# The first projection stage of a hybrid decoder layer: three output tiles instead of two beside the loads of x

## The chip, the cores and the metric

The kernel runs on one core of a Trainium2 chip. The core has a matrix engine (TensorE, PE in the profile), a vector engine (VectorE, DVE), a scalar engine (ScalarE, ACT), a general engine (GpSimd, POOL) and a queue engine (SyncE, SP). Transfers between HBM and the on-chip memory (SBUF) are issued by SP, ACT or POOL and carried out by 16 DMA engines. TensorE writes its results to PSUM, a small memory of eight banks, from where ACT and DVE read them. The metric is the device time of one execution in microseconds (us).

## The reference

One decoder layer: 16 meta tokens are put in front of 512 tokens, so that 528 positions of 1024 channels go in; 512 come out, in float32. What matters here is its first step, the normalization and the input projection, and what the first state-space group takes from it.

```python
h = jnp.concatenate([meta, x], axis=1)            # 528 x 1024
u = rmsnorm(h, mix_norm_w[i])                     # h * rsqrt(mean(h*h) + eps) * w
proj = u @ w_in[i]                                # 1024 x 9248 weights
u_pool = proj[..., OFF_POOL:OFF_Z]
z      = proj[..., OFF_Z:OFF_XBC]
xbc    = proj[..., OFF_XBC:OFF_DT]                # x (2048), B (1024), C (1024)
dt_raw = proj[..., OFF_DT:OFF_GATE]               # 32 heads
gates  = jax.nn.sigmoid(proj[..., OFF_GATE:] + b_gate[i])
...
xbc = jax.nn.silu(causal_depthwise_conv(xbc, conv_w, conv_b))
dt  = jax.nn.softplus(dt_raw + dt_bias)
...  # pooling branch, state-space scan over chunks of 128, gated merge, w_o, squared-ReLU MLP
out = rmsnorm(h, final_norm_w)
```

## The kernel before, in words

**Layout.** Positions run along the free axis: x comes in transposed as `in_xT`, eight tiles `xt[k]` of 128 channels by 528 positions (264 KB each). The weights lie in HBM as a list of blocks of 128 by 1024 float32 (512 KB), in the order in which the kernel takes them; a block of the input projection is one output tile, 128 output channels, with its eight contraction pieces of 128 columns side by side. One vector table, `in_vec` (128 by 234, 117 KB), holds all small per-channel numbers; its first eight columns are `mix_norm_w`.

**Split operands.** Each float32 operand of a matmul is split in two: ACT makes a rounded high part (`xh`, `whi`) and DVE the rest (`xl`, `wlo`). A product then takes three matmuls: high by high (line 149), high weight by low x (line 150), low weight by high x (line 152). `block_part` loads a range of columns of a block on SP's queue and splits it (lines 79 and 80). Three tiles of raw weights (tag `raw`) and four pairs of split weights can be live.

**First stage (lines 182 to 251).** x isn't normalized yet: `x_split` (lines 203 and 204) multiplies it by `mix_norm_w` only, and the results are multiplied by the row scale `rsb` afterwards (`first_raw`, line 378). While the eight tiles `xt[k]` arrive, TensorE accumulates two output tiles of group 0, B and C, in two-bank PSUM tiles `pB` and `pC` (the pool `psa`, two such tiles): step k takes 12 matmuls of 264 or 258 columns. Their weights come in column ranges 0 to 256, 256 to 512 and 512 to 1024. Before the first data TensorE is kept at work by `WARM` = 9 matmuls on a tile of ones (line 196). `dt_step` (line 212), four contraction pieces for the 32 dt columns, runs behind k = 3 and behind k = 7. The squares of x are summed in `q` beside it.

**Behind it.** dt is gathered (`pdv`, line 258), the sums of squares are taken over channels (`pn`, line 275) and turned into the row scale `rsb` (lines 279 to 295), which the softplus chain for dt, the two first-stage results and all later products of unnormalized x wait for. TensorE goes on with the rest of group 0: the tiles 0 and 1 of x (lines 390 and 391), z (`pz`), and four gate tiles (`pgp`). z is taken out of PSUM by DVE with the row scale (line 402). Then `norm_u` has made the normalized, split `uh` and `ul` (lines 353 to 355), and the groups follow. One-bank PSUM tiles come from the pool `psb` (four tiles): `pdt`, `pdv`, `pn`, `pb1`.

**Order.** The framework's planner sets the order of the work on each engine. It goes through the program with a model of times of its own: of the instructions that its model holds to be ready, an engine takes the one that stands first in the program. Each engine then works its list off in that order, so an instruction that waits holds up those behind it on its engine. The load of the activation tables of ACT stands right ahead of ACT's first ACTIVATE.

Of the kernel before, what the change touches and what calls it, by code (L numbers as in the profile page):

```python
# [9 lines left out]
F32 = mybir.dt.float32  # L10
F32R = mybir.dt.float32r
AF = mybir.ActivationFunctionType
ALU = mybir.AluOpType

P = 128
# [3 lines left out]
L = SEQ + NM  # L19
HALF = L // 2  # L20
NK = D // P
# [13 lines left out]
V_MIX, V_BG, V_PS, V_CW, V_CB, V_DS, V_SN, V_MN, V_DTB, V_AL = (  # L35
    0, 8, 24, 32, 160, 192, 208, 224, 232, 233)
# [6 lines left out]
MERGE = (0, 4, 1, 5, 2, 6, 3, 7)  # L43

WO_ORDER = [(q, i) for q in ("b11", "b12", "b22") for i in range(2)]
WARM = 9


@with_exitstack
def kernel(ctx: ExitStack, tc, xT, x, w, vec, fnw, out):  # L50
    nc = tc.nc
    act, dve, pe, pool = nc.scalar, nc.vector, nc.tensor, nc.gpsimd

    const = ctx.enter_context(tc.tile_pool(name="const", bufs=1, side="left"))
# [8 lines left out]
    def block_tiles():  # L63
        b = nblk[0]
        nblk[0] += 1
        return (b, wp.tile([P, 1024], F32, tag="raw", name=f"raw{b}", bufs=3),
                wp.tile([P, 1024], F32R, tag="whi", name=f"whi{b}"),
                wp.tile([P, 1024], F32R, tag="wlo", name=f"wlo{b}"))

    def block_load(t, c):  # L70
        nc.sync.dma_start(t[1][:, c], w[t[0], :, c])

    def block_part(t, c):
        block_load(t, c)
        block_split(t, c)

    def block_split(t, c):
# [24 lines left out]
    make_identity(nc, ident)  # L102
    ones_r = const.tile([P, P], F32R, name="ones_r")
    ones_f = const.tile([P, P], F32, name="ones_f")
    dve.memset(ones_f, 1.0)
    dve.tensor_copy(ones_r, ones_f)
    tri = const.tile([P, P], F32, name="tri")
    pool.affine_select(out=tri, in_=ones_f, compare_op=ALU.is_ge, fill=0.0, base=0,
                       pattern=[[1, P]], channel_multiplier=-1)
# [3 lines left out]
    eps = const.tile([P, 1], F32, name="eps")  # L113
    dve.memset(eps, EPS)
    vs = const.tile([P, V_N], F32, name="vs")
    nc.scalar.dma_start(vs, vec)

    def col(off, i, n=P):
        return vs[:n, off + i : off + i + 1]
# [19 lines left out]
    def psum2(name):  # L139
        return psa.tile([P, 1024], F32, tag="mm", name=name)  # L140

    def psum1(name):
        return psb.tile([P, 512], F32, tag="s", name=name)

    def proj_step(outs, k, wblk, rhs):

        wh, wl = (t[:, k * P : (k + 1) * P] for t in wblk)
        for o, c in outs:
            pe.matmul(o, wh, rhs[0][k][:, c], start=k == 0, stop=False)  # L149
            pe.matmul(o, wh, rhs[1][k][:, c], start=False, stop=False)  # L150
        for o, c in outs:
            pe.matmul(o, wl, rhs[0][k][:, c], start=False, stop=k == NK - 1)  # L152
# [5 lines left out]
    def wide(ps, skip=0):  # L158

        h = (L - skip) // 2  # L160
        runs = [(ps[:, 512 - h : 512], slice(skip, skip + h)),
                (ps[:, 512 : 512 + h], slice(skip + h, L))]
        return runs, ps[:, 512 - h : 512 + h]

    def narrow(ps):
        return [(ps, slice(NM, L))]
# [3 lines left out]
    xt = [pre.tile([P, L], F32, name=f"xt{k}") for k in range(NK)]  # L170

    xh = [pre.tile([P, 64 + SEQ], F32R, name=f"xh{k}")[:, 64 - NM :] for k in range(NK)]
    xl = [pre.tile([P, 64 + SEQ], F32R, name=f"xl{k}")[:, 64 - NM :] for k in range(NK)]
# [3 lines left out]
    X, U = (xh, xl), (uh, ul)  # L177
    H = HEADS
# [2 lines left out]

    HF = (slice(0, HALF), slice(HALF, L))
    pdt = [psum1(f"pdt{i}") for i in range(2)]
    pB, pC = psum2("px0_16"), psum2("px0_24")
    (runsB, viewB), (runsC, viewC) = wide(pB), wide(pC, NM - 4)
    b = nblk[0]
    nblk[0] += 1
    wdt = pre.tile([P, NK, H], F32, name="wdt")
    wB, wC = block_tiles(), block_tiles()
    e32 = pre.tile([P, H], F32, name="e32")  # L190
    dve.tensor_tensor(e32, ident[:, :H], ident[:, H : 2 * H], op=ALU.add)
    for c in (2, 3):
# [1 line left out]

    for n in range(WARM):
        pe.matmul(pdt[1].rearrange("p (a b) -> p a b", a=4), ones_r,
                  ones_r.unsqueeze(1).to_broadcast([P, 4, P]), start=True, stop=True)

    def x_load(k):
        nc.sync.dma_start(xt[k], xT[:, k, :])  # L200

    def x_split(k):
        act.activation(xh[k], xt[k], AF.Copy, scale=col(V_MIX, k))
        dve.scalar_tensor_tensor(xl[k], xt[k], col(V_MIX, k), xh[k].bitcast(F32),
                                 op0=ALU.mult, op1=ALU.subtract)

    def dt_step(kb):

        for i, run in enumerate(HF):
            for c in range(4):  # L210
                k = kb + c
                pe.matmul(pdt[i][c * H : (c + 1) * H, :HALF], wdt[:, k, :], xt[k][:, run],
                          start=kb == 0, stop=kb == 4, skip_group_check=True)

    def bc_step(k):
        proj_step(runsB, k, wB[2:], X)
        proj_step(runsC, k, wC[2:], X)

    x_load(0)
    x_split(0)  # L220
    for t in (wB, wC):
        block_part(t, slice(0, 256))
    x_load(1)
    bc_step(0)
    x_split(1)
    x_load(2)
    for t in (wB, wC):
        block_part(t, slice(256, 512))
    bc_step(1)
    def square(k):  # L230
        if k == 0:
            act.activation(q, xt[k], AF.Square)
        else:
            s = pre.tile([P, L], F32, tag="sq", name=f"sq{k}", bufs=2)
            act.activation(s, xt[k], AF.Square)
            dve.tensor_tensor(q, q, s, op=ALU.add)

    for k in range(2, NK):
        if k > 2:
            x_load(k)  # L240
        x_split(k)
        if k == 2:
            nc.sync.dma_start(wdt.rearrange("p k h -> p (k h)"), w[b, :, : NK * H])
            dve.tensor_tensor(wdt, wdt, vs[:, V_MIX : V_MIX + NK].unsqueeze(2).to_broadcast([P, NK, H]), op=ALU.mult)
        if k == 4:
            for t in (wB, wC):
                block_part(t, slice(512, 1024))
        bc_step(k)
        if k % 4 == 3:
            dt_step(k - 3)  # L250
        square(k - 2)
    dts_ = pre.tile([P, L], F32, name="dtp")
    for i, run in enumerate(HF):
        act.copy(dts_[:, run], pdt[i][:, :HALF])
# [34 lines left out]
    for i in range(2):  # L289
        pb = psum1(f"pb1_{i}")  # L290
        c = slice(3 * i, 3 * i + 3)
# [14 lines left out]
    for c in range(4):  # L306
        r = slice(c * H, (c + 1) * H)
# [19 lines left out]
    for c in (slice(0, P), slice(P, W)):  # L327
        n = c.stop - c.start
# [29 lines left out]
    def conv(dst, src, ct):  # L358
        n = dst.shape[-1]
        e = src.shape[-1] - n  # L360
        act.activation(dst, src[:, e:], AF.Identity, bias=col(V_CB, ct), scale=col(V_CW, ct * 4 + 3))
        for j in range(1, 4):
            o = max(0, j - e)
            dve.scalar_tensor_tensor(dst[:, o:], src[:, e + o - j : e + n - j],  # L364
                                     col(V_CW, ct * 4 + 3 - j), dst[:, o:], op0=ALU.mult, op1=ALU.add)
        act.activation(dst, dst, AF.Silu)
# [5 lines left out]
        zt = gc.tile([P, 2, SEQ], F32, tag="zt", name=f"zt{g}", bufs=1)  # L372
        return xc, bt, ct, zt

    def first_raw(name, ps, skip):
        r = pre.tile([P, L - skip], F32, tag="raw0", name=f"raw0_{name}", bufs=4)
        act.copy(r, ps)
        dve.tensor_tensor(r, r, rsb[:, skip:], op=ALU.mult)
        return r

    def group_proj(g, cur, gate=None):

        first = g == 0
        xc, bt, ct, zt = cur
        for dst, t, skip in ((bt, 16 + g, 0), (ct, 24 + g, NM - 4), (xc[:, 0, :], 2 * g, 0),
                             (xc[:, 1, :], 2 * g + 1, 0)):
            if first and (dst is bt or dst is ct):
                view = viewB if dst is bt else viewC
            else:
                runs, view = wide(psum2(f"px{g}_{t}"), skip)  # L390
                proj(runs, block(), X if first else U)
            conv(dst, first_raw(t, view, skip) if first else view, t)
            yield
        if gate is not None:
            gate_pool(gate)
            yield
        ps = psum2(f"pz{g}")
        for i in range(2):
            proj(narrow(ps[:, i * SEQ : (i + 1) * SEQ]), block(), X if first else U)
        zf = zt.rearrange("p i t -> p (i t)")  # L400
        if first:
            dve.tensor_tensor(zt, ps.rearrange("p (i t) -> p i t", i=2),
                              rsb[:, NM:].unsqueeze(1).to_broadcast([P, 2, SEQ]), op=ALU.mult)
            act.activation(zf, zf, AF.Silu)
        else:
            act.activation(zf, ps, AF.Silu)
        yield
# [251 lines left out]
    for d in range(NK):  # L659
        ps = psum2(f"psl{d}")[:, :SEQ]  # L660
# [97 lines left out]
    first = []  # L758
    for n, d in enumerate(MERGE):
# [6 lines left out]
        ps = psum2(f"pup{d}")[:, :SEQ]  # L766
        wh, wl = block()
        for i, k in enumerate(ks):
            c = slice(k * P, (k + 1) * P)
# [294 lines left out]
    c = NC - 1  # L1064
# [172 lines left out]
```

## Time and profile before

| | us |
|---|---|
| median of 3 runs (lowest to highest) | 1023.1 (1022.98 to 1023.2) |
| the profiled execution's own time | 1023.79 |
| its span, from the first to the last instruction | 1021.8 |
| PE busy in that span | 1013.0 |
| DVE, ACT busy | 739.7, 550.6 |

A row of the timeline has the start in us, the length in us (of all its instructions, where it stands for several), the engine, the line, the operation with the tiles it writes and reads, its shape, how many there are, and in brackets how long the engine had stood idle before it and for whom. Matmuls are pipelined: one of them takes longer than the distance to the next one, and the distance is what adds up.

### The profile page before, as it was taken

What the parts mean: (1) busy time and instruction counts of PE and PEld (TensorE: products, weight loads), DVE (VectorE), ACT (ScalarE), POOL (GpSimd) and SP (SyncE); (2) the same over time, 40 slices, a digit from 0 to 9 for tenths busy, and PEclk for the clock granted to TensorE, in tenths of its full rate; (3) what the DMA queues carried; (4) which work ended last, traced back from release to release, by engine and by line L of the source; (5) the groups of instructions that cost most, each with busy time, mean ns of one, the idle gap of its engine ahead of it and who ended that gap; (6) DMA issues with size and microseconds to landing.
All of it is one profiled execution on the core that took longest, in us unless ns stands there. A gap on an engine that the chain in (4) does not pass through costs nothing.

```text
span 1021.8 us, 14071 instructions
## 1 busy us (share of the span) xinstructions
PE 1013.0 (99%) x5697; PEld 872.7 (85%) x5697; DVE 739.7 (72%) x988; ACT 550.6 (54%) x729; POOL 10.0 (1%) x24
## 2 busy tenths in 40 slices
PE   9999999999999999999999999999999999999997
PEld 7889888999889998988899888888888888888886
DVE  7987796877836677978765456986686686776866
ACT  8664959495727329473244342475545455454444
POOL 0000000000000000000000001000000000000000
PEclk9999999999999999999999999999999999999999
DMA  7252141505233321514532333224323323324112
GB/s 244 83 164 83 43 145 42 166 21 165 71 95 124 103 91 34 163 26 142 186 103 83 104 104 127 79 93 155 104 83 109 118 82 114 96 101 124 42 42 83
DMA packets 29713, 105.62 MB, mean 103 GB/s; under 512 B 3345, under 2 KB 4689, under 8 KB 28625
## 3 DMA queue, kind: packets, MB, share of 16 engines
q1 hardware_dynamic: 26928, 92.75, 28.1%
q0 software_dynamic: 2000, 11.08, 3.1%
q8 instruction: 45, 0.74, 0.3%
q10 hardware_dynamic: 720, 0.91, 0.3%
q14 instruction: 20, 0.16, 0.0%
HBM read 102.55 MB, written 2.16 MB: 102 GB/s over the span
## 4 chain that ended last, share of the span: by engine, by line
PE 98%; DMA 1%; DVE 1%; ACT 0%; issue 0%; SPq 0%; ACTq 0%
PE px L149 6%; PE px L150 6%; PE px L152 6%; PE pf L98 6%; PE pf L96 6%; PE pf L97 6%; PE alpha L986 3%; PE alpha L988 3%; PE alpha L987 3%; PE pz L149 3%; PE pz L150 3%; PE pz L152 3%; PE py L500 2%; PE pso L96 2%; PE pp L150 2%; PE pp L152 2%
## 5 line engine op out<-in xcount | busy, mean ns | idle before, releaser
L79 ACT CAST whi<-raw 128x1024 fp32r<-128x1024 f32 (+1 forms) x134 | 136.0, 1024 | 232.6 <-PE pf L97 58.8
L80 DVE TENSOR_TENSOR wlo<-raw,whi 128x1024 fp32r<-128x1024 f32 (+1 forms) x134 | 159.0, 1189 | 121.0 <-ACT whi L79 113.7
L149 PE MATMUL px<-uh,whi 128*128 128x264 f32 (+1 forms) x448 | 121.0, 290 | 0.7 <-DVE ct L364 0.7
L150 PE MATMUL px<-ul,whi 128*128 128x264 f32 (+1 forms) x448 | 119.2, 286 | 0.0
L96 PE MATMUL pf<-vh,whi 128*128 128x512 f32 x256 | 99.8, 390 | 0.0
L98 PE MATMUL pf<-vh,wlo 128*128 128x512 f32 x256 | 99.6, 389 | 0.0
L97 PE MATMUL pf<-vl,whi 128*128 128x512 f32 x256 | 99.6, 389 | 0.0
L152 PE MATMUL px<-uh,wlo 128*128 128x264 f32 (+1 forms) x448 | 90.8, 284 | 0.0
L149 PEld LDWEIGHTS px<-uh,whi 128*128 128x128 f32 x448 | 84.6, 189 | 2.7 <-issue 2.4
L150 PEld LDWEIGHTS px<-ul,whi 128*128 128x128 f32 x448 | 84.9, 189 | 0.4 <-issue 0.2
L152 PEld LDWEIGHTS px<-uh,wlo 128*128 128x128 f32 x448 | 69.4, 188 | 0.3 <-issue 0.3
L748 DVE TENSOR_TENSOR slo<-b,shi 128x1024 fp32r<-128x1024 f32 x35 | 42.8, 1222 | 31.6 <-ACT shi L747 31.6
L747 ACT CAST shi<-b 128x1024 fp32r<-128x1024 f32 x35 | 36.8, 1050 | 51.8 <-PE pf L97 36.5
L97 PEld LDWEIGHTS pf<-vl,whi 128*128 128x128 f32 x256 | 48.1, 188 | 10.0
L98 PEld LDWEIGHTS pf<-vh,wlo 128*128 128x128 f32 x256 | 48.0, 188 | 10.0
L96 PEld LDWEIGHTS pf<-vh,whi 128*128 128x128 f32 x256 | 48.0, 188 | 9.9
L986 PE MATMUL alpha<-shi,hh 128*128 128x512 f32 x140 | 54.6, 390 | 0.0
L987 PE MATMUL alpha<-slo,hh 128*128 128x512 f32 x140 | 54.5, 389 | 0.0
L988 PE MATMUL alpha<-shi,hl 128*128 128x512 f32 x140 | 54.5, 389 | 0.0
L813 DVE TENSOR_TENSOR ht<-ht,alpha 128x1024 f32<-128x1024 f32 x35 | 42.6, 1217 | 6.1 <-PE alpha L988 6.1
L149 PE MATMUL pz<-uh,whi 128*128 128x512 f32 x112 | 44.0, 393 | 0.0
L150 PE MATMUL pz<-ul,whi 128*128 128x512 f32 x112 | 43.8, 391 | 0.0
(409 smaller groups left out, 2434.2 us busy)
## 6 DMA issues: line engine op xcount, KB each, us to landing
raw<-in_w SPq DMA_DIRECT2D x128, 512.0 KB, 3.6
b<-in_w SPq DMA_DIRECT2D x28, 512.0 KB, 3.5
abc<-acs_d POOLq DMA_DIRECT2D x8, 1024.0 KB, 7.5
wob<-in_w SPq DMA_DIRECT2D x8, 512.0 KB, 4.5
xt<-in_xT SPq DMA_DIRECT2D x8, 264.0 KB, 5.5
ht<-in_x POOLq DMA_DIRECT2D x4, 512.0 KB, 7.0
w<-in_w SPq DMA_DIRECT2D x4, 512.0 KB, 3.4
out_dram<-out SPq DMA_DIRECT2D x4, 320.0 KB, 2.4
```

Source lines behind the costliest of these rows:

```text
L79: act.copy(hi[:, c], raw[:, c])
L80: dve.tensor_tensor(lo[:, c], raw[:, c], hi[:, c].bitcast(F32), op=ALU.subtract)
L96: pe.matmul(ps, ah, bh, start=first, stop=False)
L97: pe.matmul(ps, ah, bl, start=False, stop=False)
L98: pe.matmul(ps, al, bh, start=False, stop=last)
L149: pe.matmul(o, wh, rhs[0][k][:, c], start=k == 0, stop=False)
L150: pe.matmul(o, wh, rhs[1][k][:, c], start=False, stop=False)
L152: pe.matmul(o, wl, rhs[0][k][:, c], start=False, stop=k == NK - 1)
L748: dve.tensor_tensor(lo, src, hi.bitcast(F32), op=ALU.subtract)
L986: pe.matmul(ps[t], a[0], wh[:, cs], start=f, stop=False, skip_group_check=True)
L987: pe.matmul(ps[t], a[0], wl[:, cs], start=False, stop=False, skip_group_check=True)
L988: pe.matmul(ps[t], a[1], wh[:, cs], start=False, stop=l, skip_group_check=True)
```

## The change: what it does

- A third output tile, tile 0 of x in group 0, is accumulated in the first stage together with B and C, in two one-bank tiles `pX` of `psb`. The x tiles of group 0 that were left for later are then only tile 1; `first_raw` takes a list of views, since the third tile lies in two banks.
- The weights of the three tiles come in ranges of one, one, two and four contraction pieces (64, 64, 128 and 256 KB each), at k = 0, 1, 2 and 4. The first three ranges are issued on ACT's queue, the others on SP's.
- The first x tile is loaded and split in two halves of 264 positions.
- `mix_norm_w` comes as a tile `vm` of its own (4 KB), first on ACT's queue; the whole table `vs` is loaded behind the first weight ranges.
- The load of the dt weights moves to k = 4, and both `dt_step`s behind k = 7.
- The tile of ones is set directly instead of being copied, and `WARM` goes from 9 to 7.

```diff
-WARM = 9
+WARM = 7
...
-    def block_load(t, c):
-        nc.sync.dma_start(t[1][:, c], w[t[0], :, c])
-
-    def block_part(t, c):
-        block_load(t, c)
+    def block_part(t, c, eng=None):
+        (eng or nc.sync).dma_start(t[1][:, c], w[t[0], :, c])
         block_split(t, c)
...
+    dve.memset(ones_r.bitcast(F32), 1.0)
     dve.memset(ones_f, 1.0)
-    dve.tensor_copy(ones_r, ones_f)
...
     vs = const.tile([P, V_N], F32, name="vs")
-    nc.scalar.dma_start(vs, vec)
+    vm = const.tile([P, NK], F32, name="vm")
+    nc.scalar.dma_start(vm, vec[:, V_MIX : V_MIX + NK])
...
-    pB, pC = psum2("px0_16"), psum2("px0_24")
+    pB, pC, pX = psum2("px0_16"), psum2("px0_24"), [psum1(f"px0_0{i}") for i in range(2)]
...
+    runsX = [(pX[i][:, :HALF], HF[i]) for i in range(2)]
...
-    wB, wC = block_tiles(), block_tiles()
+    wBCX = [block_tiles() for _ in range(3)]
...
-    def x_load(k):
-        nc.sync.dma_start(xt[k], xT[:, k, :])
+    def x_load(k, c=slice(0, L)):
+        nc.sync.dma_start(xt[k][:, c], xT[:, k, c])
...
+    def x_split(k, c=slice(0, L)):
+        act.activation(xh[k][:, c], xt[k][:, c], AF.Copy, scale=vm[:, k : k + 1])
+        dve.scalar_tensor_tensor(xl[k][:, c], xt[k][:, c], vm[:, k : k + 1], xh[k][:, c].bitcast(F32),
                                  op0=ALU.mult, op1=ALU.subtract)
...
+    PARTS = {0: slice(0, P), 1: slice(P, 2 * P), 2: slice(2 * P, 4 * P), 4: slice(4 * P, 8 * P)}
...
-    for k in range(2, NK):
-        if k > 2:
-            x_load(k)
-        x_split(k)
-        if k == 2:
+    for k in range(NK):
+        for c in HF if k == 0 else (slice(0, L),):
+            x_load(k, c)
+        if k in PARTS:
+            for t in wBCX:
+                block_part(t, PARTS[k], nc.scalar if k == 0 else nc.sync)
+        if k == 0:
+            nc.scalar.dma_start(vs, vec)
+        if k == 4:
             nc.sync.dma_start(wdt.rearrange("p k h -> p (k h)"), w[b, :, : NK * H])
...
-        bc_step(k)
-        if k % 4 == 3:
-            dt_step(k - 3)
-        square(k - 2)
+        for c in HF if k == 0 else (slice(0, L),):
+            x_split(k, c)
+        for t, runs in zip(wBCX, (runsB, runsC, runsX)):
+            proj_step(runs, k, t[2:], X)
+        if k >= 2:
+            square(k - 2)
+    for kb in (0, 4):
+        dt_step(kb)
...
-    def first_raw(name, ps, skip):
+    def first_raw(name, views, skip):
         r = pre.tile([P, L - skip], F32, tag="raw0", name=f"raw0_{name}", bufs=4)
-        act.copy(r, ps)
+        n = (L - skip) // len(views)
+        for i, o in enumerate(views):
+            act.copy(r[:, i * n : (i + 1) * n], o)
         dve.tensor_tensor(r, r, rsb[:, skip:], op=ALU.mult)
...
-            if first and (dst is bt or dst is ct):
-                view = viewB if dst is bt else viewC
+            if first and t != 1:
+                views = [viewB] if dst is bt else [viewC] if dst is ct else [o for o, _ in runsX]
```

More of the change, by code (lines that the diff above doesn't have):

```diff
@@ L197 @@
                   ones_r.unsqueeze(1).to_broadcast([P, 4, P]), start=True, stop=True)
-    def x_load(k):
[L200 to L204, printed above, removed]
+    def x_load(k, c=slice(0, L)):
[3 more added lines that the diff above has]
+        dve.scalar_tensor_tensor(xl[k][:, c], xt[k][:, c], vm[:, k : k + 1], xh[k][:, c].bitcast(F32),
                                  op0=ALU.mult, op1=ALU.subtract)
@@ L213, in dt_step @@
                           start=kb == 0, stop=kb == 4, skip_group_check=True)
[L215 to L229, printed above, removed]
+    PARTS = {0: slice(0, P), 1: slice(P, 2 * P), 2: slice(2 * P, 4 * P), 4: slice(4 * P, 8 * P)}
     def square(k):
@@ L236, in square @@
             dve.tensor_tensor(q, q, s, op=ALU.add)
-    for k in range(2, NK):
-        if k > 2:
-            x_load(k)
-        x_split(k)
-        if k == 2:
[L243 to L247, printed above, removed]
-        bc_step(k)
-        if k % 4 == 3:
-            dt_step(k - 3)
-        square(k - 2)
+    for k in range(NK):
[7 more added lines that the diff above has]
+        if k == 4:
+            nc.sync.dma_start(wdt.rearrange("p k h -> p (k h)"), w[b, :, : NK * H])
+            dve.tensor_tensor(wdt, wdt, vm.unsqueeze(2).to_broadcast([P, NK, H]), op=ALU.mult)
+        for c in HF if k == 0 else (slice(0, L),):
[6 more added lines that the diff above has]
+        dt_step(kb)
     dts_ = pre.tile([P, L], F32, name="dtp")
@@ L391, in group_proj @@
                 proj(runs, block(), X if first else U)
-            conv(dst, first_raw(t, view, skip) if first else view, t)
+                views = [view]
+            conv(dst, first_raw(t, views, skip) if first else view, t)
             yield
```

## The prediction, written before the changed kernel was run

> **What bounds the kernel now.** I read the page's first part, then what TensorE (PE) waited for, then the timeline of the first 55 us.
>
> ```profile
> span 1021.8 us, 14071 instructions
> PE 1013.0 (99%) x5697; PEld 872.7 (85%) x5697; DVE 739.7 (72%) x988; ACT 550.6 (54%) x729; POOL 10.0 (1%) x24
> ...
> PE pdt L196 <- DVE ones_r L106: 1.5, 1, 1.5
> PE px L149 <- DVE ct L364: 0.7, 1, 0.7
> PE px L150 <- DVE xl L204: 0.4, 1, 0.4
> PE px L149 <- ACT xh L203: 0.2, 1, 0.2
> PE py L500 <- issue: 0.2, 1, 0.2
> ```
>
> TensorE bounds it. The change removes no product, so it can gain only where TensorE waits, or works on nothing useful, at the head. The list of waits shows 0.6 us in the first stage, but a busy PE isn't a PE at its pace; starts show more.
>
> ```profile
> 1.51 0.79 PE L196 MATMUL pdt<-ones_r 128*128 128x512 f32 x1 [1.51 <-DVE ones_r L106]
> ...
> 4.23 0.98 PE L196 MATMUL pdt<-ones_r 128*128 128x512 f32 x2
> 4.66 0.79 PE L196 MATMUL pdt<-ones_r 128*128 128x512 f32 x2
> 5.55 0.69 PE L149 MATMUL px<-xh,whi 128*128 128x264 f32 x2
> ...
> 13.24 1.10 PE L212 MATMUL pdt<-xt,wdt 128*32 128x264 f32 x16
> ...
> 15.83 0.28 PE L149 MATMUL px<-xh,whi 128*128 128x264 f32 x1
> ...
> 18.73 0.28 PE L149 MATMUL px<-xh,whi 128*128 128x264 f32 x1
> ...
> 20.26 1.10 PE L212 MATMUL pdt<-xt,wdt 128*32 128x264 f32 x16
> 21.29 0.39 PE L149 MATMUL px<-xh,whi 128*128 128x264 f32 x1
> ...
> 28.60 0.28 PE L149 MATMUL px<-xh,whi 128*128 128x264 f32 x1
> ...
> 35.17 0.40 PE L149 MATMUL pz<-xh,whi 128*128 128x512 f32 x1
> ...
> 53.34 0.39 PE L149 MATMUL pgp<-xh,whi 128*128 128x512 f32 x1
> ```
>
> Steps 5 and 6 of B and C take 18.73 - 15.83 = 2.90, so a fed step is 1.45 us. The first four, from 5.55 to the first dt step at 13.24, take 7.69 where 5.80 would do: **1.89 us lost**, all to late x and weights. A tile of 264 columns takes (35.17 - 28.60) / 9 = 0.73 per contraction piece, so a step of three tiles is 2.18, and a dt step is 21.29 - 20.26 = 1.03.
>
> ```profile
> 0.81 0.41 ACTq L116 DMA_DIRECT2D vs<-in_vec  x1
> 1.25 0.89 SPq L71 DMA_DIRECT2D raw<-in_w  x2
> 1.25 1.28 ACT L313 ACT_TABLE_LOAD   x1 [1.25 <-PEq L1229]
> ...
> 2.18 0.91 SPq L200 DMA_DIRECT2D xt<-in_xT  x2
> ...
> 4.37 0.20 ACT L313 ACTIVATE ea<-vs 128x1 f32<-128x1 f32 x1 [1.84 <-DMA vs<-in_vec]
> 4.48 0.72 ACT L203 ACTIVATE xh<-xt,vs 128x528 fp32r<-128x528 f32 x1
> 5.11 0.70 ACT L79 CAST whi<-raw 128x256 fp32r<-128x256 f32 x2
> ...
> 10.12 1.41 ACT L203 ACTIVATE xh<-xt,vs 128x528 fp32r<-128x528 f32 x2 [0.93 <-DMA xt<-in_xT]
> ...
> SPq L243 <- DMA vs<-in_vec: 0.3, 1, 0.3
> ...
> 0.80:4.40 3.60, 2.89 (x7) 2.31 (x8) 0.52 (x3) 1.31 (x2) 0.74 (x3) 1.00 0.68 193
> 4.40:12.40 8.00, 7.27 (x46) 5.98 (x45) 6.11 (x16) 6.82 (x14) 0.00 (x0) 1.00 1.02 343
> ```
>
> The start: ACT waits for the vector table until 4.37, then makes `xh` and the first `whi`, and PE begins 0.04 us behind the first cast (5.11 + 0.40). From 4.4 to 12.4 us the transfers run at 343 GB/s with the DMA engines full: there x and the weights of B and C are bound by the transfers, while the three-tile step asks for less per us of PE.
>
> **The change part by part.**
>
> *Third tile beside the loads.* PE does the same matmuls, 0.73 per piece, earlier instead of later: no cost. The stage becomes 8 x 2.18 = 17.44 us. Bytes: 2.16 MB of x, 1.57 of weights, 0.25 of tables. 0.69 MB has come by 4.4 us (3.6 x 193), then 343 GB/s. Through x3 and the weights of k = 0 to 2 it is 2.0 MB, there at 8.2 us; through the weights of k = 4 3.05 MB, at 11.3; all 4.0 MB at 14. PE wants k = 3 at about 5.7 + 3 x 2.18 = 12.2 and k = 4 at 14.4. So the 1.89 us goes, and no transfer takes its place unless the smaller pieces move at under three quarters of that rate.
>
> ```profile
> 5.50:22.00 16.50, 15.82 (x133) 13.59 (x134) 15.44 (x29) 15.21 (x26) 0.00 (x0) 1.00 0.75 253
> ...
> L79 ACT CAST whi<-raw 128x512 fp32r<-128x512 f32 x2 | 1.2, 615 | 0.0
> ...
> L79 ACT CAST whi<-raw 128x256 fp32r<-128x256 f32 x3 | 1.1, 398 | 0.0
> ```
>
> DVE and ACT had 15.4 and 15.2 us of work from 5.5 to 22.0, and in it are all splits of x, B and C, the squares and the splits of the next blocks, tile 0 of x among them. So the new stage's share fits under 17.44, with little room.
>
> *Start.* ACT now issues five transfers. All have no inputs, so the planner can put them ahead of every ACTIVATE; the table load stood right behind ACT's issue before, and I take it to stand behind the fifth. SP's issues come every (2.18 - 1.25) / 2 = 0.465 us, so ACT's end at 0.81 + 5 x 0.465 = 3.13 and the load at 4.41. A cast of 128 columns is estimated at 0.29 (0.398 less half of the step from 256 to 512), `xh` of half a tile at 0.51, with the next start 0.41 behind. PE begins at 4.41 + 0.41 + 0.29 + 0.04 = 5.15.
>
> But the load of `wdt`, which needs nothing of `vs`, waited on SP for the landing of `vs`: it was the ninth transfer, and `vs` the first. If a ninth waits for the first to land, the issue of `vs`, ninth or tenth now, waits on ACT for `vm` or the first half of x, and the table load, every split and the first matmul wait behind it.
>
> ```profile
> DMA to landing us min/median/max: 2.3/2.4/2.6
> ...
> DMA to landing us min/median/max: 3.2/4.2/6.0
> ```
>
> These are the output stores on SP and the weight loads of the head. `vm` would land between 0.81 + 2.3 = 3.1 and 0.81 + 3.2 = 4.0, against the issue at 2.67: 0.45 to 1.35 us. It is tiny and first, so nearer to the stores: PE begins at 5.6. Between 5.15 and 5.6 I take **5.4: 0.15 earlier than now**. Ends: 4.3, where the seven warm-ups end (1.51 to 4.66 is 3.15 us for seven, from 1.15 on); and 6.9, with the late landing and three casts (0.2 each) ahead of `xh`.
>
> [...]
>
> *First step.* After the first matmul ACT has four pieces to make and DVE five, at 0.2 to 0.4 us each, against 2.18 us of PE: they keep just ahead, unless the order differs. I take 0.3 us of waits, between 0 and the 0.52 that steps 0 and 1 could have lost at most (a quarter of the 1.89 each is 0.47).
>
> *Warm-ups and the ones tile.* Removing two costs nothing if they only bridge to the first data; what they also do is in the clock rival. *dt behind* moves 2 x 1.03 us and takes none; the load of `wdt` then has until 23 us. *Two halves of x, split `vs`, `pX` in one-bank tiles*: a few more instructions, in the pieces above. SP is moved past nothing that PE waits for later: it issues ahead of the data throughout.
>
> **Sum.** -1.89 (lost steps) -0.15 (start) +0.3 (first step) = -1.74. The profiled execution of 1023.79 (span 1021.8 and 2.0 around) becomes 1022.05. It lay 0.7 above the median; against 1023.1 the forecast is **1021.35, I say 1021.3**.
>
> **Rivals.**
>
> 1. *Early start.* The table load runs while the transfers come, or `vs` isn't held: PE begins between 4.3 and 5.0, say 4.5. For it: `vs`, that ACT waited 1.84 us for, is no longer needed, and half of x and 64 KB come before 0.69 MB do. Against it: ACT's list. 1021.35 - 0.9 = 1020.4.
>
> 2. *Late start.* `vs` holds ACT until the first half of x has landed (3.2 us), or casts come first: PE begins at 6.2, and most of what the loads no longer cost is paid at the start. 1021.35 + 0.8 = 1022.2.
>
> 3. *The clock doesn't open in time.* The warm-ups start 0.43 us apart (4.23 to 4.66), but the last two end at 5.21 and 5.45, 0.24 apart: PE's pace doubled between 4.7 and 5.2, some 3.4 us after the first. Seven warm-ups from 1.15 end at 4.3, before that, and PE then idles for about 1 us. If the count begins anew with the first data, 3.4 us of real work goes at half pace and 1.7 us is lost: 1023.05, no gain. Against it: most of the time is still filled, and what matters may be just the time since the first matmul. [...]
>
> 4. *The scale chain comes too late: slower.*
>
> ```profile
> 21.80 0.66 ACT L254 COPY dtp<-pdt 128x264 f32<-128x264 f32 x2
> ...
> 22.91 1.10 PE L275 MATMUL pn<-ones_f,q 128*88 128x1 f32 x12
> ...
> 27.83 0.66 ACT L295 COPY rsb<-pb 128x264 f32<-128x264 f32 x2 [2.58 <-PE pb L293]
> ...
> 45.64 1.23 DVE L80 TENSOR_TENSOR wlo<-raw,whi 128x1024 fp32r<-128x1024 f32 x1
> ...
> 47.19 1.22 DVE L402 TENSOR_TENSOR zt<-pz,rsb 128x1024 f32<-128x1024 f32 x1
> ```
>
> With `pdt` and `pX` all four tiles of `psb` are held until dt is copied: `pn` starts not at 22.91 but at 5.4 + 0.3 + 17.44 + 2.06 + 0.66 and some 0.4 for `pdv`, 26.3, and the row scale follows 3.4 us later than now. DVE's queue behind it ends with z out of PSUM at 48.41; the second gate, which takes that PSUM tile, starts at 53.34, 4.9 later. With PE 1.74 ahead, 3.4 + 1.74 - 4.9 leaves a stall of 0.2. DVE does one or two block splits before the scale instead of behind it (1.2 each), which covers that, so I put it at nothing. If instead two splits more come ahead (2.4), the stall is 2.7: 1024.0. It makes the kernel slower than before from a stall of 1.74 on, and by over 0.2% from 3.8.
>
> **How the numbers follow.** 0.2% is 2.05 us, about what a measurement of this kernel can tell from no change: 1021.05 and 1025.15 are the bounds. The forecast, 1020.9 to 1021.8, has 0.40, of which 0.13 lies below 1021.05; the early start 0.25; the late start 0.14; the clock 0.10; the chain 0.11, of which 0.06 is beyond 1025.15. Faster: 0.13 + 0.25 = 0.38. Slower, with 0.02 for what I don't see: 0.08. Same: 0.54. The range takes in the early start down to PE at 4.3 less a little (1020.0) and the others up to the clock's 1023.1 with some of the chain: 1020.0 to 1023.4.
>
> **What would show it.** The table load behind ACT's five issues and the first `px` matmul near 5.4 show the start; a load at 1.3 or a start by 4.6 shows rival 1. Steps of 2.18 from the second on, no wait of `xh` for `xt` behind 8 us, and `pz` starting at 33.4 show the stage. 264-column matmuls 0.22 apart at the start mean rival 3; a wait of `pgp` or of a block behind `zt` means rival 4. A program that starts PE at 5.4 and has its first z matmul later than 34.5 would make me wrong in the stage itself.

## The result and the profile after

The changed kernel takes 1036.43 us (median of 4 runs, 1036.09 to 1036.5); the kernel before, on the same chip, 1023.15 (1022.98 to 1023.82). The ratio is 1.0128 with a 95% interval of 1.011 to 1.0145: 13 us slower, where 1.8 us less was forecast.

The page of the changed kernel, its first lines and three groups of matmuls (busy time in us, mean length of one in ns, idle time before):

```profile
span 1034.8 us, 14092 instructions
...
PE 1025.1 (99%) x5695; PEld 872.3 (84%) x5695; DVE 740.2 (72%) x994; ACT 552.9 (53%) x737; POOL 9.9 (1%) x24
...
L147 PE MATMUL px<-uh,whi 128*128 128x264 f32 (+1 forms) x448 | 121.1, 290 | 0.7 <-DVE ct L356 0.7
...
L93 PE MATMUL pf<-vh,whi 128*128 128x512 f32 x256 | 101.5, 396 | 0.0
...
L982 PE MATMUL alpha<-slo,hh 128*128 128x512 f32 x140 | 55.4, 396 | 0.0
```

The same groups on the page of the kernel before:

```profile
L149 PE MATMUL px<-uh,whi 128*128 128x264 f32 (+1 forms) x448 | 121.0, 290 | 0.7 <-DVE ct L364 0.7
...
L96 PE MATMUL pf<-vh,whi 128*128 128x512 f32 x256 | 99.8, 390 | 0.0
L987 PE MATMUL alpha<-slo,hh 128*128 128x512 f32 x140 | 54.5, 389 | 0.0
```

TensorE is busy 12.1 us longer with the same products. The change touches neither `pf` nor `alpha`: they are products of the last layers, hundreds of microseconds behind it. Each of them lasts 6 to 7 ns longer, while the products of 264 columns with `uh` have not changed. Nor have those of 512 columns with `uh`, before and after:

```profile
L149 PE MATMUL pz<-uh,whi 128*128 128x512 f32 x112 | 44.0, 393 | 0.0
...
L147 PE MATMUL pz<-uh,whi 128*128 128x512 f32 x112 | 43.9, 392 | 0.0
```

So the length of the product isn't what sets the slower ones apart. The distance from one matmul to the next is seen in a stretch in which TensorE has no gap. The stretch from 700 to 900 us of TensorE alone (length, busy time with the number of matmuls, clock, DMA share, GB/s), before:

```profile
700.00:900.00 200.00, 200.00 (x884) 1.00 0.33 103
```

and after, with the stretch from 4.4 to 12.4 us that the prediction quoted for the kernel before (there all five engines have a column, PE first; the last three numbers are again clock, DMA share and GB/s):

```profile
700.00:900.00 200.00, 200.00 (x859) 1.00 0.33 100
...
4.40:12.40 8.00, 6.03 (x42) 5.25 (x42) 5.69 (x19) 6.77 (x17) 0.00 (x0) 1.00 0.87 261
```

200 us for 884 matmuls is 226 ns each, for 859 it is 233, at the same granted clock of 1.00. That is where the time went, and no wait shows it: the list of TensorE's waits is as short as before.

```profile
PE pdt L195 <- DVE ones_r L102: 1.1, 1, 1.1
PE px L147 <- ACT whi L76: 1.1, 1, 1.1
PE px L148 <- DVE xl L203: 0.8, 1, 0.8
PE px L147 <- DVE ct L356: 0.7, 1, 0.7
```

The stage itself, from the timeline of the changed kernel, TensorE first, then ACT and SP:

```profile
5.58 0.39 PE L147 MATMUL px<-xh,whi 128*128 128x264 f32 x1 [1.11 <-ACT whi L76]
...
12.15 0.39 PE L148 MATMUL px<-xl,whi 128*128 128x264 f32 x1 [0.85 <-DVE xl L203]
...
14.07 0.28 PE L147 MATMUL px<-xh,whi 128*128 128x264 f32 x1
...
25.06 1.99 PE L211 MATMUL pdt<-xt,wdt 128*32 128x264 f32 x32
...
35.46 0.39 PE L147 MATMUL pz<-xh,whi 128*128 128x512 f32 x1
```

```profile
3.17 0.33 ACTq L232 DMA_DIRECT2D vs<-in_vec  x1
3.53 1.28 ACT L202 ACT_TABLE_LOAD   x1 [3.53 <-DMA vm<-in_vec]
```

```profile
2.18 2.37 SPq L71 DMA_DIRECT2D raw<-in_w  x3
4.59 0.43 SPq L199 DMA_DIRECT2D xt<-in_xT  x1
```

The first three steps take 14.07 - 5.58 = 8.49 us where 6.54 would do, so 1.95 are lost, as much as the 1.89 that the change was to save. z begins at 35.46 instead of 35.17. The head has thus lost 0.3 us, and some 12.7 come behind it.

### The profile page after: what moved, and what is told of

Read it like the earlier page. It is cut to its first block, busy times and chain, and to the rows that moved or that the text cites. A ratio compares the mean times of both kernels' runs of the same rounds, so it can differ in the third digit from the quotient of the medians.

```text
span 1034.8 us, 14092 instructions
## 1 busy us (share of the span) xinstructions
PE 1025.1 (99%) x5695; PEld 872.3 (84%) x5695; DVE 740.2 (72%) x994; ACT 552.9 (53%) x737; POOL 9.9 (1%) x24
## 3 DMA queue, kind: packets, MB, share of 16 engines
q10 hardware_dynamic: 1296, 1.11, 0.3%
## 4 chain that ended last, share of the span: by engine, by line
PE 98%; DMA 1%; DVE 1%; ACT 0%; issue 0%; ACTq 0%; SPq 0%
PE px L147 6%; PE px L148 6%; PE px L150 6%; PE pf L94 6%; PE pf L93 6%; PE pf L95 6%; PE alpha L982 3%; PE alpha L983 3%; PE alpha L981 3%; PE pz L150 3%; PE pz L147 3%; PE pz L148 3%; PE py L495 2%; PE pso L93 2%; PE pp L150 1%; PE pp L148 1%
## 5 line engine op out<-in xcount | busy, mean ns | idle before, releaser
L76 ACT CAST whi<-raw 128x1024 fp32r<-128x1024 f32 (+3 forms) x139 | 136.5, 993 | 233.1 <-PE pf L94 61.2
L77 DVE TENSOR_TENSOR wlo<-raw,whi 128x1024 fp32r<-128x1024 f32 (+3 forms) x139 | 159.5, 1152 | 128.5 <-ACT whi L76 128.5
L150 PE MATMUL pz<-uh,wlo 128*128 128x512 f32 x112 | 44.0, 393 | 0.0
## 6 DMA issues: line engine op xcount, KB each, us to landing
abc<-acs_d POOLq DMA_DIRECT2D x8, 1024.0 KB, 6.9
```

The lines of the kernel that those rows point to most:

```text
L76: act.copy(hi[:, c], raw[:, c])
L77: dve.tensor_tensor(lo[:, c], raw[:, c], hi[:, c].bitcast(F32), op=ALU.subtract)
```

## The experiments

### Where the 12 us come from: the position of a 32-byte tile

`vm` is allocated behind `vs` in the pool `const`, which lies at the left end of SBUF. It takes 32 bytes of each partition, and all tiles that are allocated behind it on the left side move up by 32: the split weights `whi`, `wlo`, `shi`, `slo`, also `uh` and `ul`. The tiles on the right side, such as `vh`, `vl`, `hh`, `hl` and `yh`, stay. In the layout of the program `whi` starts at byte 27104 before and 27136 after, `vh` at 180192 in both.

**pad32**, the kernel before with such a tile that nothing uses:

```diff
     vs = const.tile([P, V_N], F32, name="vs")
+    const.tile([P, 8], F32, name="pad")
```

> The kernel before, with an unused tile of 32 bytes per partition behind the vector table, so that everything allocated behind it on that side of SBUF lies 32 bytes higher, as in the changed kernel; no instruction is changed. Theory A (the address shift slows the 512-column products from 0.227 to 0.2335 us apart wherever only one operand moved): the first 250 us as before, then the same drift, 12.4 us in all: 1035.5. Theory B (the slower pace comes with the changed first stage or the changed order, not with addresses): 1023.1.

Measured: 1035.87 us (1035.63 to 1036.14), ratio 1.0123, interval 1.0106 to 1.014. Its groups and its stretch:

```profile
L96 PE MATMUL pf<-vh,whi 128*128 128x512 f32 x256 | 101.5, 396 | 0.0
L988 PE MATMUL alpha<-slo,hh 128*128 128x512 f32 x140 | 55.4, 396 | 0.0
```

```profile
700.00:900.00 200.00, 200.00 (x859) 1.00 0.33 100
```

An unused tile gives the whole slowdown of the products, to the number of matmuls in the stretch.

**vm_elsewhere**, the changed kernel with `vm` on the right side, in bytes taken from a pad there, so that all matmul operands lie as before (except `q`, the sums of squares, which has 12 small products and lies 32 bytes lower):

```diff
-    vm = const.tile([P, NK], F32, name="vm")
-    nc.scalar.dma_start(vm, vec[:, V_MIX : V_MIX + NK])
...
-    pre.tile([P, 24], F32, name="x_pad")
+    pre.tile([P, 16], F32, name="x_pad")
...
     q = pre.tile([P, L], F32, name="q")
+    vm = pre.tile([P, NK], F32, name="vm")
+    nc.scalar.dma_start(vm, vec[:, V_MIX : V_MIX + NK])
```

> The changed kernel, with the small tile vm on the other side of SBUF, taken out of an unused tile there (24 to 16 columns), so that all matmul operands lie where they lay before. Theory A: the drift is gone and the head's 0.5 us are what is left: 1036.4 - 12.4 = 1024.0, 512-column products 0.227 us apart in the MLP. Theory B: 1036.4.

Measured: 1024.13 us (1023.11 to 1024.45), ratio 1.0007, interval 0.9998 to 1.0017.

```profile
L93 PE MATMUL pf<-vh,whi 128*128 128x512 f32 x256 | 99.8, 390 | 0.0
```

Both directions agree: the position costs 12.3 to 12.6 us, and the rest of the change about 0.8 us, which the interval doesn't tell from nothing.

**Which property of the position?** Four more pads on the kernel before. pad64 and p128 have 64 and 128 bytes on the left side (`[P, 16]` and `[P, 32]` in place of `[P, 8]`). pad32_both has 32 on the left, and 32 on the right, which move the right side down; both_same has 32 on the left and 480 on the right:

```diff
     vs = const.tile([P, V_N], F32, name="vs")
+    const.tile([P, 8], F32, name="pad")
...
     m1p = ctx.enter_context(tc.tile_pool(name="m1p", bufs=1, side="right", reuse_waits="tile"))
+    m1p.tile([P, 120], F32, name="pad_r")
```

(pad32_both: `[P, 8]` there.)

> The kernel before, with an unused tile of 64 bytes at the same place. Theory A with a period of 64 bytes: as before, 1023.1. Theory A with a period of 128 bytes or more: slow, about 1035. Theory B: 1023.1 too, so this run tells only about the period.

> The kernel before, with 32 unused bytes on both sides of SBUF: weights and halves of the MLP's operands (split weights on one side, split activations on the other) both move, one up by 32, the other down by 32. If what counts is how the two operands of a product lie to each other modulo 64 bytes: 1023 to 1025. If what counts is the address of the weights alone: 1035.

> The kernel before with 32 bytes per partition put in on the left side (split weights move up by 32) and 480 on the right side (the activations, vh, yh, hh, move down by 480): each operand lies elsewhere than before, but the distance between the two operands of a product changes by 512. Theory R (what counts is the distance between stationary and moving operand, with a period that divides 512): products as before, pf about 227 ns apart, 1023.2 us. Theory P (what counts is each operand's own position, and the one before happened to be a good one for the weights): 234 ns for pf, about 1035.

> The kernel before with 128 bytes per partition put in on the left side only. If the relation of the operands has a period of 128 bytes: 1023.2 us, pf 227 ns apart. If the period is longer (256 or 512) or the good position is a single one: 1032 to 1036, pf 233 to 235.

| | left moves | right moves | distance `whi` to `vh`, bytes | us | `pf`, `alpha`, mean ns |
|---|---|---|---|---|---|
| before | 0 | 0 | 153088 = 299 x 512 | 1023.1 | 390, 389 |
| pad32 | +32 | 0 | 32 less | 1035.87 | 396, 396 |
| pad64 | +64 | 0 | 64 less | 1034.0 | 395, 395 |
| pad32_both | +32 | -32 | 64 less | 1032.38 | 396, 391 |
| p128 | +128 | 0 | 128 less | 1034.55 | 395, 395 |
| both_same | +32 | -480 | 512 less | 1023.32 | 390, 389 |

pad64, pad32_both, p128 and both_same were run once each; the 9 to 11.4 us by which the first three are slower are far more than the 1.5 us within which all runs of the kernel before lie.

The groups of pad32_both, then of both_same:

```profile
L96 PE MATMUL pf<-vh,whi 128*128 128x512 f32 x256 | 101.4, 396 | 0.0
L989 PE MATMUL alpha<-slo,hh 128*128 128x512 f32 x140 | 54.8, 391 | 0.0
```

```profile
L96 PE MATMUL pf<-vh,whi 128*128 128x512 f32 x256 | 99.8, 390 | 0.0
L989 PE MATMUL alpha<-slo,hh 128*128 128x512 f32 x140 | 54.5, 389 | 0.0
```

In both_same both operands lie elsewhere than before and only their distance is again a multiple of 512, and the full pace is back: 884 matmuls in the stretch from 700 to 900 us, as before, with `whi` where pad32 has it (859). So for `pf` and `alpha` it is how the two operands lie to each other that counts, and not where either lies by itself. A period of 64 bytes fell with pad64 (395 ns), one of 128 with p128 (395 ns). The two distances that are multiples of 512, 153088 and 152576 bytes, have the full pace (390 and 389 ns); whether 256 would do wasn't tried.

The distance modulo 512 doesn't explain all of it. `alpha` in pad32_both lost 2 ns where at the same distance in pad64 it lost 6. And the products of `uh` with `whi` have both operands on the left side, at distances that are 64 or 320 bytes off a multiple of 512 in every one of these layouts: their 512-column products (`pz`) start 229 ns apart before and after alike, between the 226 and the 233. Why the distance matters no run shows.

### Why the head gains nothing

With the position mended, the forecast of about 1021.3 was still missed by 2.8 us. Two suspects stood in the trace of vm_elsewhere, TensorE's timeline:

```profile
5.74 0.59 PE L145 MATMUL px<-xh,whi 128*128 128x264 f32 x1 [1.27 <-ACT whi L76]
...
8.59 0.42 PE L146 MATMUL px<-xl,whi 128*128 128x258 f32 x1
8.81 0.39 PE L145 MATMUL px<-xh,whi 128*128 128x258 f32 x1
9.02 0.29 PE L146 MATMUL px<-xl,whi 128*128 128x258 f32 x1
9.16 0.40 PE L148 MATMUL px<-xh,wlo 128*128 128x258 f32 x2
```

TensorE stood idle for 1.27 us behind the warm-ups, and until 9.0 its matmuls were 0.22 us apart, nearly twice the later 0.12. The granted clock doesn't show it; in the stretch from 7 to 8 us (five engines, then clock, DMA share, GB/s) it reads 1.00:

```profile
7.00:8.00 1.00, 1.00 (x7) 1.00 (x6) 0.95 (x4) 1.00 (x4) 0.00 (x0) 1.00 0.87 301
```

**warm10** fills the gap (`WARM` 7 to 10, on vm_elsewhere).

> The changed kernel with vm on the other side (operands where they lay before), and 10 warm-up matmuls in place of 7, so that TensorE is at work up to the first real matmul. In the execution profiled without this, the first 20 real matmuls stood 0.22 us apart until 8.8 us and 0.12 behind. Theory C (the idle 1.3 us behind seven warm-ups now and then keep TensorE at half pace): matmuls 0.12 apart from the start, and up to 0.8 us less than the 1024.1 without it: 1023.3 to 1023.8. Theory D (the pace costs nothing, because the steps wait for weights and x anyway): 1024.1.

Measured: 1023.43 us, ratio 1.0002 (0.9993 to 1.0011). A gap of 0.48 us was left, the pace was full from 7.0 on, and z began at 34.69 instead of 35.41: 0.7 us less at the head. From the first product to the dt step the stage still takes 24.29 - 5.69 = 18.60 us where 17.44 would do.

**wide_pieces** and **vs_late** have fewer transfers ahead of the first products. wide_pieces (on vm_elsewhere):

```diff
-    PARTS = {0: slice(0, P), 1: slice(P, 2 * P), 2: slice(2 * P, 4 * P), 4: slice(4 * P, 8 * P)}
+    PARTS = {0: slice(0, 2 * P), 2: slice(2 * P, 4 * P), 4: slice(4 * P, 8 * P)}
...
-        for c in HF if k == 0 else (slice(0, L),):
+        for c in (slice(0, L),):
```

> The changed kernel with vm on the other side, x's first tile in one transfer again and the first two column ranges of the three weights in one (128 KB each): four transfers fewer. Theory E (a transfer of these two queues waits for the landing of the eighth before it, so that the small pieces starve steps 0 to 2): the load of the third x tile is issued before 4 us instead of at 5.0, the steps 1 and 2 take 2.2 to 2.4 us, and the kernel gains 1.0 to 1.9 us over the 1024.1 without it: 1022.2 to 1023.1. Rival F (the splits on ACT and DVE, not the transfers, set the pace of the first steps): within 0.3 of 1024.1.

> The changed kernel with vm on the other side, and the vector table loaded on SP's queue behind the dt weights instead of on ACT's behind the first weights. ACT then has four issues, none of which waits for a landing. The table load starts at 2.7 instead of 3.5 to 3.7, and the first matmul at 4.8 to 5.0 instead of 5.6 to 5.75. If the start counts in full: 1023.3. If the later steps wait for their weights in any case: 1024.1.

wide_pieces took 1025.39 us, ratio 1.0023 (1.0013 to 1.0034): a miss. Its first three weight pieces land at 5.16, 6.95 and 7.17 us (4.21, 5.33 and 5.69 in the changed kernel), so TensorE waits 2.4 us for casts, 1.6 of it behind the warm-ups, and the half pace lasts until 12.0. vs_late, with the load of `vs` behind that of `wdt` on SP's queue, took 1023.61 (1022.5 to 1025.5). Its first matmul comes at 5.10, but the half pace until 10.6 in its trace eats that.

**combined** puts the weights in ranges of two, two and four pieces, all on SP's queue, keeps the first x tile in halves and `vs` late, with `WARM` = 8.

> The changed kernel with vm on the other side, all weights on SP's queue in 128-KB pieces for the first two steps (x's first tile still in halves), the vector table behind the dt weights on SP, 8 warm-ups; only vm is left on ACT's queue. ACT's table load stands behind one issue and ends at 2.6; first matmul at 4.3 to 4.7; no step of the first stage longer than 2.5 us. Gain over the kernel before: 1.2 from the start and 1.3 to 1.9 from the steps: 1020.3 to 1021.0. If the transfers themselves set the pace (343 GB/s at most), the later steps give back the start: 1022.

Measured: 1023.08 us (1022.97 to 1024.43), ratio 1.0002 (0.9993 to 1.0011), a miss; of the 11 runs six lie near 1023.0, four near 1024.2 and one between. The traced run is of the slower group, with half pace until 10.3. A third suspect stands in ACT's timeline:

```profile
0.81 0.41 ACTq L174 DMA_DIRECT2D vm<-in_vec  x1
3.13 1.28 ACT L202 ACT_TABLE_LOAD   x1 [3.13 <-DMA xt<-in_xT]
```

ACT has one transfer to issue, is done at 1.22, and loads its table only at 3.13, when x has landed. The first ACTIVATE needs two transfers, and the load stands behind the wait for one of them; in the kernel before it needed one, and the load ran at 1.25 while that was awaited. **table_early** (warm10 with `WARM` = 9) and **combined2** (combined with `WARM` = 9) put one ACTIVATE ahead that needs no transfer:

```diff
+    tl = pre.tile([P, 8], F32, name="tl")
+    act.activation(tl, ones_f[:, :8], AF.Exp)
```

> The changed kernel with vm on the right side, WARM 9, and one ACTIVATE of eight columns of the ones tile at the head, which waits for one memset alone, so that the table load can run at about 1.3 us instead of behind the first data. Theory T (the exposed table load is what delays the first matmul): the load ends by 3, the warm-ups end near 5.0, PE goes on without a gap, the first real matmul at 5.0 instead of 5.7 in warm10, and the pace is full at once: 1022.6 to 1023.2. Theory L (the landing of x and the weights sets the first three steps anyway): first matmul at 5.0 but the steps end where they did: 1023.4, as warm10.

> The same early ACTIVATE and WARM 9 on the combined version (weights in ranges of two, two and four contraction pieces, all on SP's queue, x0 in two halves, vs late). Theory T: first real matmul at 5.0 with no gap, full pace at once, so that only the fast sort of combined (1023.0) is left, less what the earlier first cast gives in steps 1 and 2: 1021.0 to 1022.0, and a narrow spread. Theory L: the first weights of 128 KB land near 5 to 6 us and still set the first steps: 1022.5 to 1023.1.

combined2: 1023.67 us (1023.33 to 1024.26), ratio 1.0005 (0.9996 to 1.0014), no gain over combined. The load runs at once, the first cast comes before the warm-ups end, and TensorE goes on without a gap at full pace:

```profile
1.25 1.28 ACT L174 ACT_TABLE_LOAD   x1 [1.25 <-PEq L1225]
2.54 0.21 ACT L174 ACTIVATE tl<-ones_f 128x8 f32<-128x8 f32 x1
3.17 0.92 ACT L204 ACTIVATE xh<-xt,vm 128x264 fp32r<-128x264 f32 x2 [0.41 <-DMA vm<-in_vec]
```

```profile
5.13 0.32 PE L145 MATMUL px<-xh,whi 128*128 128x264 f32 x1
...
23.81 1.99 PE L213 MATMUL pdt<-xt,wdt 128*32 128x264 f32 x32
...
34.21 0.39 PE L145 MATMUL pz<-xh,whi 128*128 128x512 f32 x1
...
1014.85 0.28 PE L1083 MATMUL last<-shi,hl 128*128 128x256 f32 x1
```

table_early took 1024.64, ratio 1.0013 (1.0004 to 1.0022), for another reason: with the table load early, ACT came to the issue of `vs` early too, was held there until 5.03, and the first matmul came at 6.17:

```profile
5.03 0.33 ACTq L234 DMA_DIRECT2D vs<-in_vec  x1
```

### Where combined2's microsecond goes

In combined2 z begins 0.96 us before that of the kernel before and the last matmul starts at 1014.85 instead of 1015.81. Yet the program ends 0.4 us later: from the last matmul's start to the end it takes 7.3 us instead of 6.0. Two more traces of the same program:

> The combined2 program once more, for a second trace. In the first one TensorE ended 0.97 us earlier than in the kernel before, and the last store landed 1.0 us later than there after its issue, so that nothing was left. Theory S (chance of that one execution): from the start of the last matmul to the end of the program it is 6.0 us, as in the other traces, and the time is 1022.3 to 1022.9 with the clock opened at once. Theory Y (it belongs to this program): again 7.0 to 7.5 us behind the last matmul, and 1023.5 to 1024.0.

> The same program a third time; as for the second. If one of the two shows 6.0 us behind the last matmul and the other 7.3, the landing of the last store varies from execution to execution.

Measured: 1023.24 and 1024.0 us, z at 33.59 and 34.41, and 7.3 us behind the last matmul in both. It belongs to the program. The last two output stores with their size and the us from issue to landing, in the kernel before, then in combined2:

```profile
out_dram<-out SPq DMA_DIRECT2D x1, 320.0 KB, 2.3
out_dram<-out ACTq DMA_DIRECT2D x1, 192.0 KB, 2.6
...
out_dram<-out SPq DMA_DIRECT2D x1, 320.0 KB, 3.3
out_dram<-out ACTq DMA_DIRECT2D x1, 192.0 KB, 3.5
```

The transfers from 1018 to 1021 us in combined2, with the packets and MB of one queue:

```profile
DMA packets 289, 0.53 MB, mean 178 GB/s; under 512 B 32, under 2 KB 160, under 8 KB 288
...
q14 instruction: 1, 0.01, 0.6%
```

One packet of program, 8 KB, is fetched at 1019.3, in the middle of these two stores, and they land 0.9 to 1.0 us later after their issue than in the kernel before. The other 0.4 us lie between the last landing and the end. Three kernels lengthen or shorten the program of one engine each, off the critical path: **c2_dve** with six small memsets more on DVE, **c2_act** with two more of the small ACTIVATEs, **c2_w8** with one warm-up matmul less.

```diff
-    pre.tile([P, 8], F32, name="x_pad")
+    xp = pre.tile([P, 8], F32, name="x_pad")
+    for _ in range(6):
+        dve.memset(xp, 0.0)
```

> combined2 with six small memsets more on DVE at the head, where DVE is idle: no work of the critical path changes, only DVE's program is six instructions longer. Theory Y1 (the last store is held by the 8 KB of program that come at 1019.3 in combined2, and where such a load falls hangs on the length of one engine's program; here DVE's): no program load between the last store's issue and its landing, 6.0 us from the last matmul to the end, 1022.5 to 1022.9. Theory Y2 (DVE's length doesn't matter): 7.3 us and 1023.5 to 1023.8, as combined2.

> combined2 with two more of the small ACTIVATEs at the head (0.2 us each, before the first data): ACT's program is two instructions longer. If the load at 1019.3 belongs to ACT's program, it moves and the end may become 6.0 us with 1022.5 to 1022.9; if not, 7.3 us and 1023.5 to 1023.8.

> combined2 with 8 warm-up matmuls instead of 9: TensorE's program is one matmul shorter, as in combined. The first real matmul 0.2 to 0.4 us earlier. If the load at 1019.3 belongs to TensorE's program it moves, as in combined, and the end becomes 6.0 us: 1022.3 to 1022.9; if not, 7.3 us and 1023.3 to 1023.8.

Measured: c2_dve 1022.91 us (1022.64 to 1023.21), c2_act 1023.55 (1023.31 to 1024.05), c2_w8 1023.76 (1023.51 to 1024.46). The same stretch of c2_dve:

```profile
DMA packets 288, 0.52 MB, mean 175 GB/s; under 512 B 32, under 2 KB 160, under 8 KB 288
```

and its last two stores:

```profile
out_dram<-out SPq DMA_DIRECT2D x1, 320.0 KB, 2.4
out_dram<-out ACTq DMA_DIRECT2D x1, 192.0 KB, 2.6
```

There is no program packet in that stretch, the stores land as in the kernel before, and the end comes 6.4 us behind the last matmul. With six instructions *more* the median is 0.64 and 0.85 us less than those of the other two, which were timed on the same chip, still fetch there and stay slow (combined2's own 1023.67 is from another chip). The 19 traces of this case bear it out: in the five with a fetch some 2 us behind the issue of the last stores (three of combined2, c2_act, c2_w8) the program ends 7.2 to 7.3 us behind the last matmul's start, in the other 14 it ends 6.0 to 6.4 us behind it. c2_dve's ratio to the kernel before is 0.9997 (0.9988 to 1.0006): half a microsecond less in the medians of one chip, 0.2% not reached, and not told from no change.

## Why the prediction was wrong

**What a part costs by its place: the step that wasn't there.** The prediction treated `vm` as a small transfer and asked only when it lands; for the rest it put "Two halves of x, split `vs`, `pX` in one-bank tiles" down as a few more instructions, at no cost of their own. That `vm` moves every later tile on the left side was in none of its steps or rivals. This is the wrong step: 12.3 to 12.6 of the 13 us, shown in both directions by pad32 and vm_elsewhere. "PE does the same matmuls, 0.73 per piece, earlier instead of later: no cost" holds for the moved tile of 264 columns, but the sum took the rate of all other products as given.

**Start: 5.4 forecast, 5.58 measured, by the mechanism that was forecast.** I had the table load behind ACT's five issues, and `vs` held until `vm` lands. `vm` landed at 3.15, as by the 2.3 us of the output stores; `vs` was issued at 3.17, and the load began at 3.53, right behind that issue (3.17 + 0.33). The working gave 5.6 for this case; 5.4 was the middle between it and 5.15. Rivals 1 and 2, a start by 5.0 or at 6.2, did not come. combined shows what the prediction didn't have: with a single issue the load still stood until x had landed, at 3.13 us. In the changed kernel that cost nothing, since the first half of x had landed at 2.97.

**Lost steps: -1.89 forecast, +0.15 measured.** This is the second wrong step. The stage took 25.06 - 5.58 = 19.48 us, 2.04 more than the 17.44 of full steps, where the kernel before had lost 1.89. "No transfer takes its place": 1.95 us were lost in the first three steps. The sum took 343 GB/s from the kernel before; 261 were moved from 4.4 to 12.4. "SP issues ahead of the data throughout" is wrong: its three weight issues stretch over 2.37 us and x of k = 2 goes out at 4.59. Waits of SP on earlier transfers make up 3.4 us in the first 14. In the trace of the changed kernel each of the transfers 9 to 24 of SP's and ACT's queues is issued behind the landing of the one eight before it: the ninth and tenth at 2.99 and 3.17, 0.02 us behind the landings of the first half of x (2.97) and of `vm` (3.15). The wait of the ninth transfer that the start was costed by had not been applied to SP's queue. With no more than eight in flight there, smaller pieces put fewer bytes in flight; that this is what took the rate from 343 to 261 is argued, and no run changes it alone. Fewer, larger pieces don't mend it (wide_pieces): the first cast then comes at 5.62 us (5.41 in vm_elsewhere), and ACT waits 0.97 us for the weights of the second. The third step's 0.85 us is DVE's: `xl` of k = 2 stood behind a `wlo` whose weights came late.

**z at 33.4 forecast, 35.46 measured**: 0.18 from the start, 1.74 from the stage (19.48 against 17.44 + 0.3), 0.14 behind it. combined2, at full pace, with the table loaded early and larger pieces, has it at 34.21, 33.59 and 34.41 in three executions: 0.8 to 1.6 us ahead of the kernel before, so the third tile beside the loads can pay. But even there the stage takes 18.1 to 18.9 us, 0.6 to 1.5 of them lost.

**Rival 3, the clock, given 0.10: the half pace came, at another point in each program.** In the trace of the changed kernel the pace is full by 6.7 us, in vm_elsewhere from 9.0, in wide_pieces from 12.2. It doesn't follow the length of the gap ahead of the first product (1.11, 1.27 and 1.59 us there, 0.38 in combined with half pace until 10.3, 0.48 in warm10 with half pace until 7.0); with no gap, in the three traces of combined2, c2_dve and c2_act, it is full by the fourth matmul. Why the point differs is not shown. The runs of combined lie in two groups 1.1 us apart; whether they differ in where the half pace ends is not shown either, since only a run of the slower group was traced. That the half pace is the clock is not shown: it is seen in the starts alone, and the granted clock reads 1.00.

**Rival 4, the scale chain:** no wait of `pgp` or of a block behind `zt` appears in TensorE's list. Nothing was paid, as forecast, although the copy of the row scale starts at 33.70 instead of 27.83, 5.9 us later and not 3.4.

## What to carry to other kernels

A tile added to a pool moves everything allocated behind it: note where the matmul operands lie before and after a change, and when products far from the change last one or two per cent longer with no wait, put in the same bytes as an unused tile before looking for anything else. In the head of the changed kernel the transfers 9 to 24 were issued behind the landing of the one eight before, the table load stood behind the issue of `vs` (3.53 us), and TensorE stood idle for 1.11 us ahead of its first products, so look at the transfers in flight, at the first wait of the engine that makes the operands and at the idle time of TensorE before judging such a stage. And when the matmuls end earlier and the program doesn't, look at the transfers behind the last of them.

## What the runs showed of the hardware that was not expected

- The 512-column products from 700 to 900 us, `pf` and `alpha` above all, run 226 ns apart at the two distances of `whi` to `vh` in a partition that are multiples of 512 bytes (before and both_same, 884 in the stretch). At distances 32, 64 or 128 off (pad32, pad64, p128) they run 232 to 233 ns apart (859 to 861); with 32 on both sides (pad32_both) `pf` lasts 396 ns and `alpha` 391, against 390 and 389 before. `pz` from `uh`, 64 or 320 off, runs 229 ns apart before and after.
- The activation table load (1.28 us) starts only at 3.13 us, behind the landing of x, where the first ACTIVATE needs two transfers and one issue stands ahead of it (combined); an ACTIVATE that needs none, put ahead, lets it run at 1.25 us (combined2).
- With a fetch of 8 KB of program among them the last output stores land 0.9 to 1.0 us later (3.3 and 3.5 us behind their issue in combined2, 2.3 and 2.6 in the kernel before), and six instructions more on DVE moved it away (2.4 and 2.6 us in c2_dve; 0.64 to 0.85 us in the medians of the same chip). The other fetches were not looked at.
